# Hybrid attention and mLSTM layer on one core: the first stage with transposes, gate rows fetched two heads ahead, compression blocks split straight from PSUM, compression steps between projection tiles

## The chip, the cores and the metric

The kernel runs on one core of a Trainium2 chip. The core has TensorE (PE: matmuls, with PEld loading the stationary operand beside it), VectorE (DVE), ScalarE (ACT), GpSimd (POOL) and SyncE (SP, which here only issues DMAs). The metric is the device time of one execution in microseconds; lower is better. All times below are in microseconds.

## The reference

```
h = rms_norm(x, mix_norm_pre)                       # x: 512 x 1024
q, kc, vc, ks, vs, kw, vw, gt, mq, mk, mv, mi, mf, mo = split(h @ w_in)
k_cmp, v_cmp = compress_blocks(kc, ...), compress_blocks(vc, ...)
#   blocks of 32 tokens, stride 16, + pos; silu(blocks @ w1) @ w2
o = native_sparse_attention(q, k_cmp, v_cmp, ks, vs, kw, vw, sigmoid(gt), rel_bias)
mq, mk = split(silu(causal_conv(concat(mq, mk), conv_w) + conv_b))
hm = mlstm(mq, mk, mv, mi + bias, log_sigmoid(mf + bias))   # 4 heads, gated decay
y = concat(o, sigmoid(mo) * rms_norm(hm) * mlstm_norm) @ w_out
x = x + rms_norm(y);  x = x + rms_norm(cross_attention(rms_norm(x), mem))
x = x + rms_norm(swiglu_ffn(rms_norm(x)))
```

Everything is float32, and the changed parts lie before the attention: the first norm, the product with w_in, the convolution, the compression of key and value blocks, and the mLSTM heads.

## The kernel before

Matmuls run on pairs of fp32r numbers. `split(hi, lo, src, eng)` writes the rounded high half on ACT (a copy) and the rest on DVE or POOL (a subtract); `mm3` then makes three matmuls, high by low, low by high, high by high. In the names below, whi and wlo are the halves of a projection weight, hTh and hTl those of the transposed normed input H, wah and wal those of the gate weights, w1s both halves of a piece of the compression weights, Xb both halves of the compression input.

The first stage is a block in which the order of the instructions on every engine is the written one (manual_schedule). For each of the four rows i of 128 tokens it takes the sum of squares on ACT (`square_of`), the factor rstd on DVE and POOL (`factor_of`, rs_e and rs_r), turns the row into H by eight matmuls, four to a PSUM bank bk_pn (`turn_row`, two calls), splits the banks (`parts_of`) and multiplies H by the gate and window-value weights, 24 matmuls of 288 columns to a row (bk_A, `gates_and_v(i, 0)` and `(i, 1)`). `keep_a` takes bk_A's results out. After the block comes `mlstm_v`, 96 matmuls of 512 columns (bk_mv).

After it a scheduler that works when the kernel is built, and not a fixed list, sets each engine's order: it takes the program in the order of PLAN["order"], by priority, as operands and buffers become available in its own model. In that string c0, c1 (convolution input), m0, m2 (output gate), kc, ks (keys and values), q0 are projections, and each name stands once for each of the tiles that it has. A tile is 24 matmuls into a bank bk_dT. Lk, Lv load the compression weights; Ck, Cv are steps of the compression (four matmuls of 512 columns each into bk_hb); S0 to S3 are the scores of an mLSTM head (bk_ms) and O0 to O3 its output (bk_mn, bk_mt). Every name of `PLAN["m0"]` and the like says for each tile whether POOL (p) or DVE (v) makes wlo.

Buffers are rings: the weights whi/wlo, five of the eight w1s of the keys and all w1s of the values use one of 4 buffers ("W"), the other w1s and the rows of x one of 4 ("T"), 512-column temporaries one of 16 ("G"), the large pairs such as hT one of 6 ("S"). A new writer waits until the reader of the buffer that it takes is done. PSUM has 2 banks for projection tiles, 3 for scores and bk_hb, 2 for turns, 1 for values.

`ev_conv` takes a tile of c0 or c1 out of PSUM and begins the convolution with the newest tap; `ev_mo` takes m0 and m2 tiles out (tanh) and scales them; `ev_kcvc` builds the compression input of kc's two tiles; `mlstm_scores` makes an mLSTM head's decay weights from rb, a row of rd (a DRAM scratch) broadcast to all partitions by a 256 KB DMA.

## Time and profile before

| what | value |
| --- | --- |
| median of 3 runs | 849.62 (848.80 to 850.38) |
| the profiled execution, its own time | 849.66 |
| its span, first to last instruction | 847.9 |
| mean granted TensorE clock, share of full | 0.992 |
| PE busy | 821.3 (97%), 4870 matmuls |
| DVE busy | 542.3 (64%) |
| ACT busy | 425.1 (50%) |
| POOL busy | 299.2 (35%) |

The profile is one execution; 1.8 of its own time lies outside the span. Busy shares are means over stages with different limits. A granted clock of 1.00 is 2.4 GHz and 0.50 is 1.2 GHz. Where PE idles, the trace names what it waited for. PE's matmuls overlap, so the distance between two starts is what a matmul costs, not its printed duration.

### The profile page before, as it was taken

The numbers are of one execution on the slowest core, as the hardware profiler recorded it, in microseconds if no ns is written. First come the engines' busy times: TensorE is split into PE (matmuls) and PEld (weight loads), VectorE is DVE, ScalarE is ACT, GpSimd is POOL, SyncE is SP. The second block draws the span as 40 slices with busy tenths as digits, with TensorE's granted clock in tenths as the row PEclk, the third lists the DMA queues.
The fourth block names the chain that finished last, engine by engine and source line by source line (L and its number), as shares of the span: only waits on it lengthen the run. The fifth ranks groups of instructions, "written<-read, shape, count | busy, mean of one in ns | idle before, by whom it ended". The sixth has DMA issues, their size and how long they took to land.

```text
span 847.9 us, 12708 instructions
## 1 busy us (share of the span) xinstructions
PE 821.3 (97%) x4870; PEld 707.7 (83%) x4870; DVE 542.3 (64%) x934; ACT 425.1 (50%) x840; POOL 299.2 (35%) x224
## 2 busy tenths in 40 slices
PE   8999989999999999999999999999999999999997
PEld 5977767886688978778888889999999999888885
DVE  5738696697879835843453769988877885224323
ACT  5524565858867743743452556444444444324311
POOL 2043332355537542511320111444444444323320
PEclk9999999998999999999999999999999999999999
DMA  8371323221203232251341033333333322232102
GB/s 246 95 229 63 100 66 107 99 69 50 76 1 100 94 133 73 70 179 53 137 160 50 0 125 105 121 111 111 111 113 113 108 106 100 100 100 100 49 26 75
DMA packets 67763, 83.18 MB, mean 98 GB/s; under 512 B 4368, under 2 KB 53873, under 8 KB 67702
## 3 DMA queue, kind: packets, MB, share of 16 engines
q1 hardware_dynamic: 64574, 77.97, 28.3%
q10 hardware_dynamic: 3128, 4.40, 1.6%
q8 instruction: 38, 0.62, 0.3%
q14 instruction: 23, 0.19, 0.1%
HBM read 80.24 MB, written 2.12 MB: 97 GB/s over the span
## 4 chain that ended last, share of the span: by engine, by line
PE 78%; DVE 7%; ACT 3%; issue 1%; POOL 1%; DVEq 0%; ACTq 0%; POOLq 0%
PE bk_X L1301 5%; PE bk_X L1302 5%; PE bk_X L1303 5%; PE bk_ff L286 5%; PE bk_ff L288 5%; PE bk_ff L287 5%; PE bk_dT L286 4%; PE bk_dT L287 4%; PE bk_dT L288 4%; PE bk_pv L1027 3%; PE bk_dN L287 3%; PE bk_dN L286 3%; PE bk_dN L288 3%; PE bk_Z L1301 2%; PE bk_Z L1302 2%; PE bk_Z L1303 2%
## 5 line engine op out<-in xcount | busy, mean ns | idle before, releaser
L166 ACT ACTIVATE whi<-raw 128x1024 fp32r<-128x1024 f32 (+1 forms) x80 | 76.8, 968 | 63.4 <-PE bk_dT L286 27.8
L167 DVE TENSOR_TENSOR wlo<-raw,whi 128x1024 fp32r<-128x1024 f32 x41 | 54.2, 1323 | 81.5 <-PE bk_ff L287 43.0
L167 POOL TENSOR_TENSOR wlo<-raw,whi 128x1024 fp32r<-128x1024 f32 x23 | 55.8, 2428 | 106.4 <-ACT whi L166 104.6
L166 ACT ACTIVATE wh<-raw 128x1024 fp32r<-128x1024 f32 x64 | 67.3, 1057 | 49.3 <-PE bk_X L1301 16.1
L167 POOL TENSOR_TENSOR wl<-raw,wh 128x1024 fp32r<-128x1024 f32 x19 | 55.5, 2921 | 97.5 <-ACT wh L166 70.2
L286 PE MATMUL bk_dT<-hTh,wlo 128*128 128x512 f32 x192 | 76.9, 401 | 1.1 <-DVE wlo L167 0.8
L287 PE MATMUL bk_dT<-hTl,whi 128*128 128x512 f32 x192 | 76.3, 397 | 0.0
L288 PE MATMUL bk_dT<-hTh,whi 128*128 128x512 f32 x192 | 76.1, 396 | 0.0
L167 DVE TENSOR_TENSOR wl<-raw,wh 128x1024 fp32r<-128x1024 f32 x45 | 64.6, 1440 | 9.2 <-ACT wh L166 9.2
L167 POOL TENSOR_TENSOR gs<-gf,gs 128x512 fp32r<-128x512 f32 x22 | 32.4, 1478 | 65.9 <-ACT gs L166 65.9
L1302 PE MATMUL bk_X<-A,wh 128*128 128x256 f32 x192 | 54.5, 284 | 1.0 <-DVE A L167 1.0
L1301 PE MATMUL bk_X<-A,wl 128*128 128x256 f32 x192 | 54.4, 283 | 0.4 <-ACT A L166 0.4
L1303 PE MATMUL bk_X<-A,wh 128*128 128x256 f32 x192 | 54.3, 283 | 0.0
L287 PE MATMUL bk_ff<-wlo,gs 128*128 128x512 f32 x128 | 49.8, 389 | 0.0
L288 PE MATMUL bk_ff<-whi,gs 128*128 128x512 f32 x128 | 49.6, 389 | 0.0
L1301 PE MATMUL bk_X<-AS,wl 128*128 128x256 f32 x160 | 45.6, 285 | 2.4 <-ACT u L1356 2.3
L286 PE MATMUL bk_ff<-whi,gs 128*128 128x512 f32 x128 | 47.4, 389 | 0.0
L997 POOL TENSOR_SCALAR s<-s,acf 128x128 f32<-128x128 f32 (+3 forms) x32 | 36.5, 1151 | 26.7 <-PE bk_tr L1012 15.9
L1302 PE MATMUL bk_X<-AS,wh 128*128 128x256 f32 x160 | 44.9, 281 | 0.0
L1301 PE MATMUL bk_Z<-AS,wl 128*128 128x256 f32 x160 | 44.9, 281 | 0.0
L1303 PE MATMUL bk_X<-AS,wh 128*128 128x256 f32 x160 | 44.9, 281 | 0.0
L1303 PE MATMUL bk_Z<-AS,wh 128*128 128x256 f32 x160 | 44.9, 280 | 0.0
(376 smaller groups left out, 2535.2 us busy)
## 6 DMA issues: line engine op xcount, KB each, us to landing
raw<-in_w_gate_up_dram SPq DMA_DIRECT2D x22, 1024.0 KB, 6.5
raw<-in_w_down_dram SPq DMA_DIRECT2D x11, 1024.0 KB, 4.9
raw<-in_w_xkv_dram SPq DMA_DIRECT2D x8, 1024.0 KB, 5.1
raw<-in_w_in_dram SPq DMA_DIRECT2D x7, 1024.0 KB, 5.3
raw<-in_w_out_dram SPq DMA_DIRECT2D x4, 1024.0 KB, 5.1
raw<-in_w_xq_dram SPq DMA_DIRECT2D x4, 1024.0 KB, 5.4
raw<-in_w_xo_dram SPq DMA_DIRECT2D x4, 1024.0 KB, 5.1
raw<-in_w_in_dram SPq DMA_DIRECT2D x6, 512.0 KB, 4.7
```

The costliest lines, as they stand in the source:

```text
L166: first = nc.scalar.activation(hi, src, AF.Copy)
L167: second = (eng or nc.vector).tensor_tensor(lo, src, hi.bitcast(F32), op=OP.subtract)
L286: nc.tensor.matmul(o, lhsT=wl, rhs=xh, start=start, stop=False)
L287: nc.tensor.matmul(o, lhsT=wh, rhs=xl, start=False, stop=False)
L288: return nc.tensor.matmul(o, lhsT=wh, rhs=xh, start=False, stop=stop).ins
L997: ENG[on].tensor_scalar(s[:, 0:n], s[:, 0:n], c, None, op0=OP.mult)
L1027: nc.tensor.matmul(o, lhsT=v, rhs=pTs[br][q][:, j], start=(br, j, q) == mms[0], stop=(br, j, q) == mms[-1])
L1301: nc.tensor.matmul(o, lhsT=wl[:, k, c], rhs=A.hi(n, k), start=st, stop=False, skip_group_check=True)
L1302: nc.tensor.matmul(o, lhsT=wh[:, k, c], rhs=A.lo(n, k), start=False, stop=False, skip_group_check=True)
L1303: nc.tensor.matmul(o, lhsT=wh[:, k, c], rhs=A.hi(n, k), start=False, stop=stop and k == 3, skip_group_check=True)
```

## The change

1. First stage. The row is scaled by rstd and gain in one DVE instruction (`norm_half`), and turned by a PE transpose with the identity in place of a matmul by diag(rstd). The multiplication by the gain alone (xg) and the building of the diagonal (mt) are left out. x's second row is loaded ahead of the gate weights, the third ahead of their second half. The calls stand in a new order: row 1 is turned between the two halves of row 0's gates_and_v, and the squares and factors come earlier.
2. Gate rows. The store of rd and the loads of rb go through SP's queue instead of ACT's, and rb is loaded two heads ahead (`load_rb`).
3. `ev_conv` and `ev_mo`: a DVE tensor_scalar becomes an ACT Identity with scale and bias, in ev_conv from PSUM.
4. `ev_kcvc`: Xb is split straight from PSUM with a stride of 16, four ACT copies and four DVE subtracts of 64 x 496 to a tensor, in place of eight DVE adds of 64 x 248, four ACT copies and four DVE subtracts. The position goes into the 32nd column of the block list and is added back through `fold` and `every`.
5. The value weights of the compression take two "G" buffers in place of one "W" in every second piece.
6. PLAN["order"]: two Ck stand between the tiles of m0, two before c1; Cv stand one by one between S1, m2, S2 and m2.

The diff, cut to its core:

```diff
-        "order": "c0 Lk c0 Lv kc m0 m0 Ck Ck Ck Ck c1 kc S0 O0 c1 "
-                 "S1 Cv Cv Cv Cv m2 S2 m2 O2 ks O1 ks q0 S3 q0 O3",
+        "order": "c0 Lk c0 Lv kc m0 Ck Ck m0 Ck Ck c1 kc S0 O0 c1 "
+                 "Cv S1 Cv m2 Cv S2 Cv m2 O2 ks O1 ks q0 S3 q0 O3",
...
         "w1tk": "WTWTWTWW",
-        "w1tv": "WWWWWWWW",
-        "xb": "vv",
+        "w1tv": "GWGWGWGW",
...
     nc.sync.dma_start(cc[:, 0:128], a["consts"][:, 0:128])
+    load_x(1)
     raw_a = [load_a(0)]
-    load_x(1)
+    load_x(2)
     raw_a.append(load_a(1))
-    load_x(2)
     load_x(3)
...
-    xg, dg, turned, bank_a = {}, {}, {}, {}
+    xn, factor, turned, bank_a = {}, {}, {}, {}
     def square_of(i):
-        ss = dg[i] = small([P, 1], "ss", 4)
+        ss = factor[i] = small([P, 1], "ss", 4)
         nc.scalar.activation(sgran((P, D), BF16, name="junk"), res(i), AF.Square, scale=1.0 / 32.0, accum_out=ss)
-    def gain_of(i, g):
+    def factor_of(i):
+        factor[i] = rstd_of(factor[i], 1)
+    def norm_half(i, g):
         if g == 0:
-            xg[i] = x4([P, D], name="xg")
+            xn[i] = x4([P, D], name="xn")
         c = slice(512 * g, 512 * g + 512)
-        nc.vector.tensor_tensor(xg[i][:, c], res(i)[:, c], g_in[g], op=OP.mult)
-    def factor_of(i):
-        r = rstd_of(dg[i], 1)
-        dg[i] = small([P, P], "mt1")
-        nc.vector.tensor_scalar(dg[i], ident, r, None, op0=OP.mult)
+        nc.vector.scalar_tensor_tensor(xn[i][:, c], res(i)[:, c], factor[i], g_in[g], op0=OP.mult, op1=OP.mult)
...
             kk = 4 * g + k
-            nc.tensor.matmul(b[:, 128 * k:128 * k + 128], lhsT=xg[i][:, 128 * kk:128 * kk + 128], rhs=dg[i],
-                             start=True, stop=True)
+            nc.tensor.transpose(b[:, 128 * k:128 * k + 128], xn[i][:, 128 * kk:128 * kk + 128], ident)
...
         nc.scalar.activation(g_in[1], spread[1], AF.Copy)
-        gain_of(0, 0)
+        square_of(1)
         factor_of(0)
-        turn_row(0, 0)
-        gain_of(0, 1)
-        turn_row(0, 1)
+        for g in range(2):
+            norm_half(0, g)
+            turn_row(0, g)
         warm_up(2)
-        parts_of(0, 0)
+        factor_of(1)
+        for g in range(2):
+            parts_of(0, g)
         split_a(0)
-        parts_of(0, 1)
+        norm_half(1, 0)
         split_a(1, 2, 3)
         raw_m = [load_m(0)]
+        norm_half(1, 1)
         gates_and_v(0, 0)
         for g in range(2):
-            gain_of(1, g)
+            turn_row(1, g)
+        square_of(2)
         split_a(4, 5)
-        square_of(1)
-        factor_of(1)
+        factor_of(2)
+        for g in range(2):
+            parts_of(1, g)
         split_a(6, 7)
...
         gates_and_v(0, 1)
-        square_of(2)
         for g in range(2):
-            turn_row(1, g)
-        for g in range(2):
-            gain_of(2, g)
-        for g in range(2):
-            parts_of(1, g)
+            norm_half(2, g)
         for i in range(1, NT):
             then = i + 1 < NT
-            if then:
-                factor_of(i + 1)
             gates_and_v(i, 0)
...
             done = gates_and_v(i, 1)
-            last = (done, *keep_a(i - 1))
             if i + 2 < NT:
                 square_of(i + 2)
-                for g in range(2):
-                    gain_of(i + 2, g)
+                factor_of(i + 2)
             if then:
...
                     parts_of(i + 1, g)
+            if i + 2 < NT:
+                for g in range(2):
+                    norm_half(i + 2, g)
+            last = (done, *keep_a(i - 1))
     with ExitStack() as behind:
...
     rd = dr.tile([4, 512], F32, name="rd")
-    nc.scalar.dma_start(rd, rr)
+    nc.sync.dma_start(rd, rr)
+    rbs = {}
+    def load_rb(h):
+        if h < 4:
+            rbs[h] = sgran(name="rb")
+            nc.sync.dma_start(rbs[h], rd[h:h + 1, :].to_broadcast([P, 512]))
+    for h in range(2):
+        load_rb(h)
     nc.vector.tensor_tensor(ir, ir, br_, op=OP.subtract)
...
             nc.scalar.activation(u, b, AF.Copy)
-            nc.vector.tensor_scalar(y, u, cw(c, 3), cb(c), op0=OP.mult, op1=OP.add)
+            nc.scalar.activation(y, b, AF.Identity, scale=cw(c, 3), bias=cb(c))
             for w in range(3):
...
             nc.scalar.activation(sg[c], b, AF.Tanh, scale=0.5)
-            nc.vector.tensor_scalar(sg[c], sg[c], 1.0, hn(c), op0=OP.add, op1=OP.mult)
+            nc.scalar.activation(sg[c], sg[c], AF.Identity, scale=hn(c), bias=hn(c))
         return f
...
         nc.vector.scalar_tensor_tensor(kB[r], zc[2 + h // 2][r], 0.0625, kA[r].bitcast(F32), op0=OP.mult, op1=OP.subtract)
-        rb = mgran(name="rb")
-        nc.scalar.dma_start(rb, rd[h:h + 1, :].to_broadcast([P, 512]))
+        rb = rbs[h]
         dg = mgran((P, NT, P), name="dg")
...
             sT.append(W[:, c0:c0 + n])
+        load_rb(h + 2)
         return sT
...
         n = "kv"[j]
-        Xr = [sgran((P, 8, 64), name="Xr") for _ in range(2)]
-        for X in Xr:
-            nc.gpsimd.memset(X, 0.0)
+        X = Xb[n] = slot([P, 2, 8, 2, 64], F32R, name="Xb")
+        nc.gpsimd.memset(X[:, :, :, :, 63:64].bitcast(F32), 0.0)
+        pos = posT[n].rearrange("p (q j o) -> p q j o", q=2, o=1)
+        split(X[:, :, :, 0, 31:32], X[:, :, :, 1, 31:32], pos)
+        full, to = [], []
         for kv in range(2):
             for r in range(2):
-                full = b[64 * kv:64 * kv + 64, :].rearrange("p (b j r) -> p r j b", r=2, j=8)
-                pt = posT[n][64 * r:64 * r + 64, :]
-                for q in range(2):
-                    nc.vector.tensor_tensor(Xr[q][64 * r:64 * r + 64, :, 32 * kv:32 * kv + 31],
-                                            full[:, r, :, q:q + 31],
-                                            pt[:, 8 * q:8 * q + 8].rearrange("p (j o) -> p j o", o=1).to_broadcast([64, 8, 31]),
-                                            op=OP.add)
-        Xb[n] = []
-        for X in Xr:
-            for g in range(2):
-                B = gran((P, 4, 2, 64), F32R, name="Xb")
-                split(B[:, :, 0, :], B[:, :, 1, :], X[:, 4 * g:4 * g + 4, :], engines("xb")[g])
-                Xb[n].append(B)
+                one = b[64 * kv:64 * kv + 64, r:r + 1]
+                full.append(bass.AP(tensor=one.tensor, offset=one.offset, ap=[one.ap[0], [16, 2], [2, 8], [16, 31]]))
+                to.append(X[64 * r:64 * r + 64, :, :, :, 32 * kv:32 * kv + 31])
+        for q in range(4):
+            nc.scalar.activation(to[q][:, :, :, 0], full[q], AF.Copy)
+        for q in range(4):
+            nc.vector.tensor_tensor(to[q][:, :, :, 1], full[q], to[q][:, :, :, 0].bitcast(F32), op=OP.subtract)
...
     nc.vector.tensor_tensor(fold, ident[:, 0:64], ident[:, 64:128], op=OP.add)
+    every = small([P, 1], "every", 1)
+    nc.vector.tensor_copy(every, fold[:, 31:32])
+    nc.vector.tensor_scalar(fold, fold, every, None, op0=OP.add)
...
         for s in range(8):
-            take = x4 if PLAN["w1t" + n][s] == "T" else w4
-            w = take([P, 2, 2, 256], F32R, name="w1s")
-            split(w[:, :, 0, :], w[:, :, 1, :], w1r[n, s // 4][s % 4], engines("w1" + n)[s])
+            take = PLAN["w1t" + n][s]
+            if take == "G":
+                w = [gran((P, 2, 256), F32R, name="w1s") for _ in range(2)]
+                for k in range(2):
+                    split(w[k][:, 0, :], w[k][:, 1, :], w1r[n, s // 4][s % 4][:, k], engines("w1" + n)[s])
+            else:
+                t = (x4 if take == "T" else w4)([P, 2, 2, 256], F32R, name="w1s")
+                split(t[:, :, 0, :], t[:, :, 1, :], w1r[n, s // 4][s % 4], engines("w1" + n)[s])
+                w = [t[:, k] for k in range(2)]
             for k in range(2):
                 kk = 2 * s + k
-                nc.tensor.matmul(hb[n], lhsT=Xb[n][kk // 4][:, kk % 4].rearrange("p q b -> p (q b)"),
-                                 rhs=w[:, k].rearrange("p q c -> p (q c)"), start=kk == 0, stop=kk == 15)
+                nc.tensor.matmul(hb[n], lhsT=Xb[n][:, kk // 8, kk % 8].rearrange("p q b -> p (q b)"),
+                                 rhs=w[k].rearrange("p q c -> p (q c)"), start=kk == 0, stop=kk == 15)
             if s == 7:
```

Order of the instructions. First PE in the first stage, where row 1 is turned (bk_pn is a turn of eight; bk_A is a step of three matmuls; each row names engine, line and operands). Before:

```order
L286 MATMUL bk_A<-wah,hTl 128x288
L287 MATMUL bk_A<-wal,hTh 128x288
L288 MATMUL bk_A<-wah,hTh 128x288
L491 MATMUL bk_pn<-mt_227,xg 128x128 x8
L286 MATMUL bk_A<-wah,hTl 128x288
L287 MATMUL bk_A<-wal,hTh 128x288
L288 MATMUL bk_A<-wah,hTh 128x288
```

24 bk_A matmuls precede the turn, so it stands behind both halves of row 0. After:

```order
L285 MATMUL bk_A<-wah,hTl 128x288
L286 MATMUL bk_A<-wal,hTh 128x288
L287 MATMUL bk_A<-wah,hTh 128x288
L488 MATMUL bk_pn<-cc,xn 128x128 x8
L285 MATMUL bk_A<-wah,hTl 128x288
L286 MATMUL bk_A<-wal,hTh 128x288
L287 MATMUL bk_A<-wah,hTh 128x288
```

Twelve bk_A matmuls precede it now: row 1 is turned in the middle of row 0.

Next PE at the end of m0's first tile, bk_dT, of which the last two matmuls are shown (names carry the number of the buffer; hb is a compression step, ms a score of an mLSTM head). After:

```order
L286 MATMUL bk_dT_819<-hTl_95,whi_815 128x512
L287 MATMUL bk_dT_819<-hTh_93,whi_815 128x512
L892 MATMUL bk_hb_847<-w1s_848,Xb_801 128x512 x2
L892 MATMUL bk_hb_847<-w1s_853,Xb_801 128x512 x2
L761 MATMUL bk_ms_1030<-qm_1019,kmA_1020 128x512
L761 MATMUL bk_ms_1039<-qm_1019,kmA_1020 128x384
L892 MATMUL bk_hb_847<-w1s_858,Xb_801 128x512 x2
L892 MATMUL bk_hb_847<-w1s_863,Xb_801 128x512 x2
L762 MATMUL bk_ms_1030<-qm_1019,kmB_1025 128x512
```

and behind these 24 matmuls of m0's second tile begin (bk_dT_872, whi_868). Before, this place held m0's second tile at once, and the four Ck came behind both tiles:

```order
L287 MATMUL bk_dT_864<-hTl_95,whi_860 128x512
L288 MATMUL bk_dT_864<-hTh_93,whi_860 128x512
L880 MATMUL bk_hb_892<-w1s_893,Xb_814 128x512 x2
L880 MATMUL bk_hb_892<-w1s_898,Xb_814 128x512 x2
L756 MATMUL bk_ms_1057<-qm_1044,kmA_1045 128x512
L757 MATMUL bk_ms_1057<-qm_1044,kmB_1050 128x512
L756 MATMUL bk_ms_1066<-qm_1044,kmA_1045 128x384
L757 MATMUL bk_ms_1066<-qm_1044,kmB_1050 128x384
```

So eight bk_hb and four bk_ms stand between the tiles now, and the other eight behind the second.

Last ACT ahead of whi of m2's first tile (whi_1294 before, whi_1229 after; sT, qm, kmA, hnat, mt are mLSTM work, Xb and w1s compression). Before:

```order
L709 ACTIVATE u_1174<-bk_dT_1149 128x512
L166 ACTIVATE w1s_1241<-w1_758 128x2x256
L787 ACTIVATE mt1_1105,mss_1087<-hnat_1086 128x128
L787 ACTIVATE mt1_1116,mss_1087<-hnat_1086 128x128
L166 ACTIVATE w1s_1246<-w1_763 128x2x256
L166 ACTIVATE w1s_1251<-w1_764 128x2x256
L166 ACTIVATE w1s_1256<-w1_765 128x2x256
L166 ACTIVATE w1s_1261<-w1_766 128x2x256
L166 ACTIVATE whi_1294<-raw_1292 128x1024
```

After:

```order
L769 ACTIVATE sT_1288<-rb_1059,ub_614 128x128 x3
L165 ACTIVATE w1s_1167<-w1_755 128x2x256
L821 ACTIVATE Xb_1007<-bk_dT_982 64x16x31 x4
L165 ACTIVATE w1s_1222<-w1_757 128x2x256
L168 ACTIVATE kcmp_651<-bk_cmp_932 128x2x32
L914 DMA w2_1336<-in_cmp_w2_v_dram 128x2x64
L831 ACTIVATE qm_1274<-zc_970 64x512
L793 ACTIVATE mt1_1080,mss_1062<-hnat_1061 128x128
L791 ACTIVATE hnat_1061<-bk_mn_1082,dn_1086 128x128
L165 ACTIVATE whi_1229<-raw_1227 128x1024
```

The w1s copies of the last four pieces and u of c1's second tile no longer stand ahead of it; three exps, two w1s, four Xb copies, which now read PSUM, kcmp, qm, mt and hnat do.

## Rows read from the trace of the kernel before

**Rows 1.** Busy table of the page: us, share of span, instructions.

```profile
PE 821.3 (97%) x4870; PEld 707.7 (83%) x4870; DVE 542.3 (64%) x934; ACT 425.1 (50%) x840; POOL 299.2 (35%) x224
```

**Rows 2.** Windows: from:to, length, busy PE, PEld, DVE, ACT, POOL, clock, DMA, GB/s.

```profile
58.70:143.37 84.67, 78.70 (x359) 61.01 (x357) 67.08 (x127) 46.52 (x104) 32.10 (x32) 0.98 0.31 93
...
125.00:128.40 3.40, 3.40 (x8) 1.98 (x7) 3.40 (x6) 1.68 (x3) 1.39 (x2) 0.50 0.00 0
...
193.30:200.10 6.80, 6.15 (x21) 4.47 (x20) 5.71 (x18) 6.70 (x18) 4.90 (x4) 0.50 0.36 108
```

**Rows 3.** Timeline of PE, first stage: start, duration, engine, line, operation [idle before, releaser].

```profile
17.33 0.40 PE L287 MATMUL bk_A<-wal,hTh 128*128 128x288 f32 x1 [0.77 <-POOL wal L167]
...
18.46 1.95 PE L491 MATMUL bk_pn<-mt,xg 128*128 128x128 f32 x16
...
20.93 0.40 PE L286 MATMUL bk_A<-wah,hTl 128*128 128x288 f32 x1 [0.52 <-DVE hTl L167]
...
21.16 0.29 PE L287 MATMUL bk_A<-wal,hTh 128*128 128x288 f32 x1
...
22.48 0.29 PE L288 MATMUL bk_A<-wah,hTh 128*128 128x288 f32 x1
...
34.40 0.29 PE L288 MATMUL bk_A<-wah,hTh 128*128 128x288 f32 x1
```

**Rows 4.** Timeline of PE, transposes at the end of attention's first units.

```profile
227.92 1.04 PE L254 MATMUL bk_pn<-cc,xn 128*128 128x128 f32 x8
```

**Rows 5.** Timeline of DVE and POOL, first stage.

```profile
13.19 1.89 DVE L480 TENSOR_TENSOR xg<-xin,gain 128x512 f32<-128x512 f32 x2
...
15.96 0.56 POOL L236 TENSOR_TENSOR rs_r<-rs_e,mhalf 128x1 f32<-128x1 f32 x1 [2.03 <-DVE rs_e L232]
...
16.48 1.55 POOL L167 TENSOR_TENSOR wal<-raw,wah 128x288 fp32r<-128x288 f32 x2
```

**Rows 6.** Timeline of PE, projection tiles.

```profile
58.70 0.48 PE L286 MATMUL bk_dT<-hTh,wlo 128*128 128x512 f32 x1
...
68.73 0.39 PE L287 MATMUL bk_dT<-hTl,whi 128*128 128x512 f32 x1
...
90.79 1.20 PE L880 MATMUL bk_hb<-w1s,Xb 128*128 128x512 f32 x4 [0.89 <-DVE w1s L167]
...
118.83 0.38 PE L756 MATMUL bk_ms<-qm,kmA 128*128 128x256 f32 x1 [1.75 <-DVE sT L766]
...
124.78 3.62 PE L880 MATMUL bk_hb<-w1s,Xb 128*128 128x512 f32 x8 [1.61 <-DVE w1s L167]
...
128.99 0.50 PE L286 MATMUL bk_dT<-hTh,wlo 128*128 128x512 f32 x1 [0.58 <-DVE wlo L167]
...
143.37 0.48 PE L286 MATMUL bk_dT<-hTh,wlo 128*128 128x512 f32 x1
```

**Rows 7.** Timeline of ACT, POOL and DVE, weight splits.

```profile
93.30 1.06 ACT L166 ACTIVATE whi<-raw 128x1024 fp32r<-128x1024 f32 x1 [0.30 <-PE bk_hb L880]
...
118.43 0.61 ACT L166 ACTIVATE w1s<-w 128x512 fp32r<-128x512 f32 x1
...
102.87 2.38 POOL L167 TENSOR_TENSOR wlo<-raw,whi 128x1024 fp32r<-128x1024 f32 x1 [7.70 <-ACT whi L166]
...
127.73 1.20 DVE L167 TENSOR_TENSOR wlo<-raw,whi 128x1024 fp32r<-128x1024 f32 x1
```

**Rows 8.** Window of ACT's work in the projections, columns as in rows 2.

```profile
108.74:118.43 9.69, 8.11 (x41) 6.32 (x40) 8.51 (x22) 9.06 (x25) 2.55 (x2) 1.00 0.32 77
```

**Rows 9.** Timeline of PE, start of attention.

```profile
192.35 0.44 PE L977 MATMUL bk_sc<-kA,qst 128*128 128x384 f32 x1 [1.15 <-DVE mx L981]
...
193.86 1.09 PE L698 MATMUL bk_pcT<-cc,pc 128*128 128x128 f32 x4 [0.55 <-DVE pc L695]
```

**Rows 10.** Adds of ev_kcvc by line (min/median/max ns), and ACT at rb.

```profile
L811 DVE TENSOR_TENSOR Xr<-bk_dT,chan x16: 398/410/420, 81.0 to 114.7; 64x248 f32<-64x248 f32 x16
...
132.94 0.99 ACT L764 ACTIVATE sT<-rb,ub 128x128 f32<-128x128 f32 x3 [1.82 <-DMA rb<-rd]
```

## Prediction

> **What bounds the kernel now.** I read the busy table first: TensorE (PE) is busy 97% of the span [rows 1], so whatever shortens the run must take out PE's own matmuls, its waits, or its time at the lower clock. Then windows, then PE's timeline in the two places that the change touches. The later two thirds (attention units, w_out, cross-attention, FFN) run without a wait worth naming and the change doesn't touch them.
>
> The first place is the first stage. Before the last matmul of bk_A PE runs turns (bk_pn, matmuls by diag(rstd)) and bk_A in one line. A turn of 8, two banks, listed as 16 halves, starts at 18.46 and costs about 2.0; bk_A's matmuls of 288 columns start 0.132 apart at full clock (21.16 to 22.48 in ten steps) [rows 3]. The waits are for wal, the low halves of the gate weights (0.77 before 17.33), and for hTl (0.52 before 20.93). The last bk_A begins at 34.40, ends at 34.69.
>
> The second place is the row of projection tiles from the first c0 matmul at 58.70 to the first ks matmul at 143.37 [rows 6]: 84.67, of which PE is busy 78.70, so 5.97 idle [rows 2]. The large idles stand before bk_hb (0.89, 1.61), bk_ms (1.75) and m2's first tile (0.58) [rows 6]: a tile or a compression step (Ck, Cv) waits for the split of its weights. After the last series the clock is half from 125.0 to 128.4 (0.50 for 3.4 us, so 1.7 of full clock) [rows 2]; the eight bk_hb in it take 3.62 [rows 6] where eight at full clock take 1.9: 512 columns start at most 0.233 apart (58.70 to 68.73 in 43 steps). Counted start to start, a wait is 0.1 to 0.2 longer than its printed idle, since PE also empties and refills. The nine places in which a step starts late by 0.24 or more (first at 83.87, last at 128.99) are late by 7.7 together, and the half clock adds 1.4. So **9.1 us** can be gained there.
>
> The third is the start of attention: PE waits 1.15 before 192.35 for mx and 0.55 before 193.86 for pc, both from VectorE (DVE) [rows 9], and a half-clock stretch follows from 193.3 to 200.1 (0.50) [rows 2].
>
> **The first stage.** A turn becomes eight transposes. The trace has the same 128x128 transpose later: eight in 1.04 [rows 4], about 0.11 apart; with 0.9 to 1.0 a turn against 2.0. The order rows put row 1's turn in the middle of row 0's bk_A, where PE waits for wal anyway. So behind row 0's second half only two turns are left. Before: from 18.46 to 34.69 = 16.2, which is 72 x 0.132 = 9.5, three turns of 2.0, 0.52 of wait and small change. After: 9.5 + 2 x 0.9 = 11.3. That is −4.9.
>
> Ahead of it, the last two wal (POOL, 16.48 for 1.55) stand behind rs_r at 15.96, which stood behind two gain multiplies of row 1 on DVE (13.19, 1.89 for the two, slow because POOL ran too) [rows 5]. After, row 1's factor comes earlier since x1 is loaded ahead of the gate weights, and the DVE no longer multiplies by the gain apart from the scale. Walking POOL, ACT and DVE through the new order with these durations, I get the end of wal 1.1 earlier. Sum **−6.0**, between −4.5 (the turn in the gap delays bk_A) and −6.5. Everything behind (bk_mv, its loads and splits) can follow: splits of wm lead PE by about 2.6 now, and the new order gets to them as much earlier. The moved keep_a and the removed diag costs lie under PE's bk_A.
>
> The price of the transposes is the largest unknown of this part. The row shows eight in 1.04, and the turns of now, eight ordinary matmuls of the same size, 2.0. I take the row of the transposes; should they cost what a turn costs now, two turns of 2.0 instead of 0.9 take back 2.2. The page "TensorE: Matmul & The Clock Gate" of the Trainium skill, section "Part 4: PE-mode transpose", speaks for the dear price: it gives about 275 ns for one transpose inside a kernel, by which a turn of eight would cost 2.2 and the whole sum below would be 2.6 smaller.
>
> **Compression blocks from PSUM.** Before, ev_kcvc adds the positions on DVE, 16 instructions of 0.41 [rows 10], and then splits; after, four ACT copies and four DVE subtracts a tensor read PSUM with the same stride, each over twice as many elements. No row shows an ACT copy with this stride. The DVE adds bound it: 0.4 if width costs nothing, 0.8 by doubling. I take 0.6. DVE is relieved of the adds and of eight 512-wide scales, since the conv's last tap and ev_mo's scale become ACT Identity, near 0.6 each as w1s, a copy of as many elements [rows 7]. This earns nothing by itself: what it costs ACT stands in wait 3 below. The position column, the added `every` and the two memsets are small and lie under PE's tiles. Gate rows: ACT waited 1.82 for rb before 132.94 [rows 10]; the store of rd and the loads of rb now stand on SP's queue, where they wait for DMAs only, and the weights of ks, the next load behind them, are needed some 15 us later. PE ran m2's second half at 132.94, so this earns nothing directly, at most ACT's 1.8.
>
> **Projections.** The new order and pools remove all of the 9.1 as it stands and set four new waits. Whi is 1.06 on ACT (0.95 apart), wlo 2.38 on POOL and 1.20 on DVE, w1s 0.61 on ACT [rows 7].
>
> (1) m0's second tile, now behind two Ck: its whi takes the buffer that m0's first tile frees at its end; 0.95 + 2.38 = 3.3 against 8 bk_hb (1.9) and four bk_ms (0.8): 0.6.
>
> (2) c1's first tile, behind the other two Ck: w1s 0.61, sg 0.5, whi 0.95, wlo 1.20 = 3.3 against 8 bk_hb and four small bk_ms, 2.4: 0.85.
>
> (3) m2's first tile. In the order of ACT (third place in the order rows) its whi is behind all that begins at c1's first tile's end: whi, u, zc, hid, then what before's ACT does in 9.06 from 108.74 to 118.43 [rows 8] (hnat, qm, kmA, ten exps, tanh, w1s, Xb), with larger Xb (+1.0) and two more mt and hnat (+0.9), and its own 1.06: 14.6, then 1.2 for wlo: 15.8. PE meanwhile has 48 matmuls of 512 columns (11.2) and some 16 small ones (1.8): 13.0. Wait 2.8, taken as **3.0 ± 1**.
>
> (4) m2's second tile: ACT has about 9 to 10 between the two whi, PE about 10.1 less the 1.2 of wlo: 0 to 2, taken as 1.1.
>
> Sum 5.55. A wait of 3 in the midst of busy matmuls is like what stood before the half clock at 125.0; I count one such stretch, +1.5 (1.7 at most). So 9.1 − 5.55 − 1.5 = **−2.0**.
>
> **Attention's start.** PE would arrive about 8 us earlier, but so does the DVE chain (its work is the same and DVE's backlog smaller): −0.5, between 0 and −2.
>
> **Sum.** −6.0 − 2.0 − 0.5 = −8.5. The profiled execution took 849.66, the median of three is 849.62, so it makes no difference: 849.6 − 8.5 = **841.1**.
>
> **Rivals.**
>
> (a) Nothing of waits 3 and 4 appears, since ACT gets the copies done in gaps that I counted as full. Then 1.45 of 9.1 remains: −6.0 − 7.6 − 0.5 = 835.5. For it: PE's waits before were for DVE, which is relieved. Against: the order on ACT.
>
> (b) The projections gain nothing: the same waits plus a longer half-clock stretch (as 193.3 to 200.1, 3.4 instead of 1.5) and one more short one (+1.7): 9.1 − 5.55 − 5.1 = −1.5 turns to +1.5, 849.6 − 6.0 + 1.5 = 845.1.
>
> (c) bk_mv comes before the split weights: the lead of 2.6 is used up and 2.6 of the first stage's gain is given back, 843.7. For it: wm's pieces come from ACT and DVE one at a time behind the new splits and factors, and their loads depend on buffers, not on PE alone. Against: ACT and DVE are idle between bk_A's rows.
>
> (c') Transposes cost what turns cost now: 841.1 + 2.2 = 843.3. Only the row of another stage speaks against it. (The price that the Trainium skill's page gives would come out here.)
>
> (d) Slower: half-clock stretches follow every one of the four new waits, and each is of the long kind (3.4). Nine us of gain are needed to be lost: 4 x 3.4 = 13.6 in place of 1.5 gives 849.6 − 8.5 + 12.1 = 853.2; it decides from three long ones on. For: near 193 it fell where the waits were of only 1.15 and 0.55 [rows 2, 9]. Against: the stretch from 58.70 to 143.37 has 0.98 as its mean and just one half-clock piece, though PE waits eight times in it [rows 2].
>
> (e) No part reaches the end: the first stage's gain is taken back by loads and the projections as in (b): 849.6 + 1.5 − 0.5 = 850.6.
>
> **How the numbers follow.** Forecast 0.46 (its own range 838.6 to 843.6, by the bounds of wait 3, of the clock and of the first stage); (a) 0.17; (b) 0.16; (c) 0.05; (c') 0.04; (d) 0.07; (e) 0.05. The range leaves out the ends of (a), (d) and (e): 834.5 to 846.5. A measurement of this kernel tells about 0.2%, 1.7 us, from no change; (e) is within it, (d) beyond, the rest faster, with a little of (b) moved to no change: 0.86, 0.06, 0.08.
>
> **What would show it.** The last bk_A at about 28.6 instead of 34.7; turns of 8 in about 0.9; first ks matmul near 135 (143.4 − 8); PE waits before m0's second tile on POOL wlo of 0.6, before c1's first on DVE wlo of 0.85, and before m2's first tile of about 3 behind whi, with a clock under 1.00 in the windows that follow; no ACT wait on rb; no TENSOR_SCALAR in ev_conv; Xb copies on ACT of 0.6. I am wrong if the m2 wait is absent (a), if strided copies cost over 1.5, or if bk_mv waits for its weights (c).

## The result: slower by 0.55%, and the profile after

The changed kernel takes 853.69 (median of 6 runs, 851.86 to 855.62) against 849.21 for the kernel before; the ratio is 1.0055 with an interval of 1.0038 to 1.0072. It was forecast at 841.1 with 834.5 to 846.5: wrong, and on the other side. The profiled execution of the changed kernel is its slowest, 855.62 with a span of 853.8, 6.0 more than the one of before. Counted from the start of each execution, the first c0 matmul comes 2.0 later (60.73), the first ks matmul 3.3 later (146.69), the first bk_pcT 5.7 later (199.53) and the first matmul of w_out 7.2 later; 1.3 of this comes back behind it.

The busy table of the page, as in [rows 1]:

```profile
PE 816.7 (96%) x4838; PEld 703.7 (82%) x4838; DVE 537.3 (63%) x911; ACT 432.5 (51%) x854; POOL 303.4 (36%) x225
```

PE is busy 4.6 less in a span that is 5.9 longer: it idles 37.1 instead of 26.6. First the timeline of PE in the first stage, as in [rows 3]:

```profile
15.04 0.44 PE L287 MATMUL bk_A<-wah,hTh 128*128 128x288 f32 x1
15.28 1.88 PE L488 MATMUL bk_pn<-cc,xn 128*128 128x128 f32 x8
...
20.26 0.49 PE L286 MATMUL bk_A<-wal,hTh 128*128 128x288 f32 x1 [0.54 <-POOL wal L166]
...
23.43 0.45 PE L287 MATMUL bk_A<-wah,hTh 128*128 128x288 f32 x1
...
28.40 0.37 PE L285 MATMUL bk_A<-wah,hTl 128*128 128x288 f32 x1 [2.03 <-DVE gl L508]
...
30.06 1.04 PE L488 MATMUL bk_pn<-cc,xn 128*128 128x128 f32 x8
...
33.38 0.37 PE L285 MATMUL bk_A<-wah,hTl 128*128 128x288 f32 x1 [0.71 <-DVE gl L508]
...
36.49 0.29 PE L287 MATMUL bk_A<-wah,hTh 128*128 128x288 f32 x1
```

The last bk_A begins at 36.49, not at 28.3 (its forecast end of 28.6 less its own 0.29). A turn of eight does cost what the forecast took, 1.04. But twice PE waits for gl, the last instruction of keep_a, which frees the bank that the next row's bk_A writes; keep_a now stands behind parts_of and norm_half. The last wal comes at 20.26 instead of 18. And the clock is at its lower level where it wasn't: bk_A's matmuls start 0.24 apart and the turn takes 1.88 up to 17.1 (before the change only until 12.4), and again from 20.3. POOL and ACT show why wal is late: its wah stands behind the hTh of row 1, which waits for the turn.

```profile
17.20 0.60 ACT L165 ACTIVATE hTh<-bk_pn 128x512 fp32r<-128x512 f32 x1 [0.23 <-PE bk_pn L488]
17.69 0.77 ACT L165 ACTIVATE wah<-raw 128x288 fp32r<-128x288 f32 x2
...
18.20 2.00 POOL L166 TENSOR_TENSOR wal<-raw,wah 128x288 fp32r<-128x288 f32 x2 [1.94 <-ACT wah L165]
```

Windows of the changed kernel, columns as in [rows 2], and behind them two of the kernel before that answer to the fifth and sixth:

```profile
20.30:23.70 3.40, 3.40 (x15) 3.39 (x16) 0.52 (x2) 0.00 (x0) 0.55 (x1) 0.52 0.68 198
60.73:146.69 85.96, 77.39 (x346) 61.07 (x343) 59.27 (x100) 52.02 (x112) 34.18 (x32) 0.96 0.31 95
88.00:95.00 7.00, 6.83 (x23) 5.54 (x24) 5.21 (x7) 6.42 (x18) 2.92 (x2) 0.76 0.44 116
124.00:131.50 7.50, 6.56 (x22) 5.21 (x23) 7.05 (x12) 2.97 (x8) 7.25 (x7) 0.77 0.00 0
146.69:199.53 52.84, 49.52 (x268) 41.69 (x269) 35.78 (x123) 35.84 (x96) 19.16 (x18) 0.98 0.27 80
199.53:299.96 100.43, 98.29 (x632) 78.90 (x633) 85.09 (x259) 76.05 (x208) 54.43 (x40) 0.97 0.18 59
```

```profile
143.37:193.86 50.49, 47.80 (x260) 40.32 (x260) 37.65 (x122) 32.26 (x91) 19.67 (x17) 0.99 0.27 89
193.86:292.73 98.87, 98.28 (x629) 79.12 (x629) 82.56 (x255) 76.91 (x209) 54.74 (x40) 0.97 0.19 59
```

From c0 to ks PE idles 8.57 where it idled 5.97, and there are two pieces with a lowered clock (7.0 at 0.76 and 7.5 at 0.77, 1.7 of full clock each) where there was one of 1.7. That is 4.3; the stretch grew only by 1.3, in part because 14 small matmuls of the mLSTM outputs and of the compression (six bk_mn, four bk_ht, four bk_cmp) slipped behind ks, where PE is busy 1.7 more. Taken over the three stretches up to w_out PE idles 14.0 instead of 9.3. These are the large waits of the projections, as in [rows 6], and of attention's start, as in [rows 9]:

```profile
88.17 1.61 PE L892 MATMUL bk_hb<-w1s,Xb 128*128 128x512 f32 x4 [2.73 <-ACT whi L165]
...
101.22 0.50 PE L285 MATMUL bk_dT<-hTh,wlo 128*128 128x512 f32 x1 [0.60 <-DVE wlo L166]
...
124.94 0.50 PE L285 MATMUL bk_dT<-hTh,wlo 128*128 128x512 f32 x1 [3.68 <-DVE wlo L166]
...
137.15 0.47 PE L761 MATMUL bk_ms<-qm,kmA 128*128 128x512 f32 x1 [1.22 <-DVE sT L771]
...
194.99 0.36 PE L989 MATMUL bk_sc<-kA,qst 128*128 128x256 f32 x1 [0.78 <-DVE dn L786]
...
196.95 0.44 PE L989 MATMUL bk_sc<-kA,qst 128*128 128x384 f32 x1 [1.48 <-DVE mx L993]
...
198.36 0.69 PE L989 MATMUL bk_sc<-kA,qst 128*128 128x384 f32 x1 [0.80 <-DVE mx L993]
...
201.74 1.12 PE L798 MATMUL bk_mt<-cc,hnat 128*128 128x128 f32 x4 [0.70 <-DVE hnat L797]
```

Behind the wait of 3.68 the clock falls, as the forecast had it. This wait is not ACT's alone. ACT ends whi of m2's first tile at 122.01, but DVE begins wlo only at 123.67: it is at the subtracts of Xb until 121.87, and those of w1s, kcmp and qm stand behind them, ahead of wlo.

```profile
119.14 2.73 DVE L823 TENSOR_TENSOR Xb<-bk_dT,Xb 64x496 fp32r<-64x496 f32 x4 [1.55 <-ACT Xb L821]
...
120.96 1.05 ACT L165 ACTIVATE whi<-raw 128x1024 fp32r<-128x1024 f32 x1
...
123.67 1.21 DVE L166 TENSOR_TENSOR wlo<-raw,whi 128x1024 fp32r<-128x1024 f32 x1
```

The wait of 2.73 was not in the forecast. It is put down to a whi, but this is not what Ck needs, and the load of Ck's stationary operand, Xb, begins before that whi ends at 88.16. The timelines of ACT, DVE and PEld show the chain:

```profile
82.92 2.34 ACT L821 ACTIVATE Xb<-bk_dT 64x496 fp32r<-64x496 f32 x4
...
85.29 2.73 DVE L823 TENSOR_TENSOR Xb<-bk_dT,Xb 64x496 fp32r<-64x496 f32 x4 [1.55 <-ACT Xb L821]
...
87.10 1.06 ACT L165 ACTIVATE whi<-raw 128x1024 fp32r<-128x1024 f32 x1
...
88.13 0.91 PEld L892 LDWEIGHTS bk_hb<-w1s,Xb 128*128 128x128 f32 x4 [3.13 <-issue]
```

The first of the four subtracts begins only behind the last of the four copies, the last one ends at 88.02, and PE starts 0.15 later. With Ck directly behind m0's first tile, Xb, which nobody waited for before, is late.

### The profile page after: what moved, and what is told of

It reads as the page before. It is cut to its first block, busy times and chain, and to the rows that moved or that the text cites. A ratio compares the mean times of both kernels' runs of the same rounds, so it can differ in the third digit from the quotient of the medians.

```text
span 853.8 us, 12625 instructions
## 1 busy us (share of the span) xinstructions
PE 816.7 (96%) x4838; PEld 703.7 (82%) x4838; DVE 537.3 (63%) x911; ACT 432.5 (51%) x854; POOL 303.4 (36%) x225
## 4 chain that ended last, share of the span: by engine, by line
PE 80%; DVE 10%; ACT 5%; issue 3%; POOL 2%; ACTq 0%; DVEq 0%; POOLq 0%
PE bk_X L1313 5%; PE bk_X L1314 5%; PE bk_ff L285 5%; PE bk_ff L287 5%; PE bk_ff L286 5%; PE bk_X L1315 5%; PE bk_dT L285 5%; PE bk_dT L286 4%; PE bk_dT L287 4%; PE bk_pv L1039 3%; PE bk_dN L286 3%; PE bk_dN L285 3%; PE bk_dN L287 3%; PE bk_tr L1024 2%; PE bk_Z L1313 2%
## 5 line engine op out<-in xcount | busy, mean ns | idle before, releaser
L166 DVE TENSOR_TENSOR wl<-raw,wh 128x1024 fp32r<-128x1024 f32 x45 | 66.9, 1493 | 9.1 <-ACT wh L165 9.1
L285 PEld LDWEIGHTS bk_dT<-hTh,wlo 128*128 128x128 f32 x192 | 36.5, 190 | 14.4 <-DVE wlo L166 6.2
L1314 PE MATMUL bk_X<-AS,wh 128*128 128x256 f32 x160 | 44.3, 277 | 0.0
```

The source lines that it names most:

```text
L166: second = (eng or nc.vector).tensor_tensor(lo, src, hi.bitcast(F32), op=OP.subtract)
L285: nc.tensor.matmul(o, lhsT=wl, rhs=xh, start=start, stop=False)
L1314: nc.tensor.matmul(o, lhsT=wh[:, k, c], rhs=A.lo(n, k), start=False, stop=False, skip_group_check=True)
```

## The experiments

Each ran in five rounds beside the kernel before, whose median lay between 848.86 and 849.06 in every group.

| run | median | ratio to before, interval |
| --- | --- | --- |
| first_only | 848.22 | 0.9991 (0.9976 to 1.0005) |
| first_old | 855.01 | 1.0065 (1.0052 to 1.0079) |
| keep_mid | 853.26 | 1.0044 (1.0023 to 1.0066) |
| warm4 | 854.34 | 1.0056 (1.0040 to 1.0071) |
| order_old | 849.74 | 1.0021 (1.0002 to 1.0040) |
| kc_old | 853.27 | 1.0052 (1.0035 to 1.0070) |
| ident_old | 854.83 | 1.0064 (1.0044 to 1.0084) |
| rb_old | 859.28 | 1.0119 (1.0101 to 1.0137) |
| order_m0 | 856.54 | 1.0081 (1.0054 to 1.0109) |
| order_cv | 852.13 | 1.0035 (1.0020 to 1.0050) |
| order_only | 858.26 | 1.0127 (1.0099 to 1.0154) |
| best1 | 851.57 | 1.0029 (1.0012 to 1.0045) |
| first_fix | 841.81 | 0.9917 (0.9902 to 0.9932) |
| kc_only | 856.51 | 1.0092 (1.0074 to 1.0110) |
| ident_only | 853.00 | 1.0053 (1.0037 to 1.0068) |
| rb_only | 856.06 | 1.0087 (1.0069 to 1.0106) |
| after_fix | 848.35 | 0.9996 (0.9979 to 1.0013) |
| first_keep | 844.76 | 0.9948 (0.9930 to 0.9966) |

**The first stage alone, and undone.** first_only is the kernel before with the diff's loads, norm_half, turn_row and the calls in their new order; first_old is the changed kernel without them.

> The kernel before with the new first stage alone (loads of x, transposes, new order of the calls), the rest as before. Theory A: the first stage loses by itself, about +2 at the first c0 matmul (60.7 against 58.7 in the changed kernel's trace), by the wait for keep_a's DVE gl (2.0 + 0.7) and by half clock until 17.1 and from 20.3 to 23.7: total about +2, 851. Rival B: the first stage gains as forecast where nothing else is changed (-6): 843.

> The changed kernel with the old first stage. Theory A: the loss of the first stage goes away and what the projections and attention's start lose stays (+1.3 and +2.3 in the trace): about 2 less than the changed kernel, 851.5, still slower than before. Rival B, that the later losses follow from the first stage's end (loads and buffers that come later): back to 849 or less.

Alone the first stage does nothing that can be measured; undoing it makes the changed kernel no faster, so that both forecasts for first_old were missed. The loss of 4.5 is thus not the first stage's, against theory A, and a gain of 6 isn't there either, against rival B. In the trace of first_only the same waits for gl stand (2.02 and 0.69), behind the longer one the clock is at its lower level, and its last bk_A ends at 34.8, as the one of the kernel before (34.7):

```profile
24.91 0.58 PE L286 MATMUL bk_A<-wah,hTl 128*128 128x288 f32 x1 [2.02 <-DVE gl L509]
```

```profile
24.80:28.20 3.40, 3.29 (x14) 3.30 (x15) 0.00 (x0) 0.00 (x0) 0.00 (x0) 0.50 0.03 5
```

**Its two waits.** keep_mid and warm4 are the changed kernel with

```diff
                     parts_of(i + 1, g)
+            last = (done, *keep_a(i - 1))
             if i + 2 < NT:
                 for g in range(2):
                     norm_half(i + 2, g)
-            last = (done, *keep_a(i - 1))
```

and with

```diff
-        warm_up(2)
+        warm_up(4)
         nc.scalar.activation(g_in[0], spread[0], AF.Copy)
```

> The changed kernel with keep_a moved between parts_of and norm_half. Theory A: gl is done before the multiplies by rstd and gain, the wait of 2.0 before bk_A at 28.4 shrinks to about 0.6 (norm_half's 1.4 is out of the chain), the one at 33.4 stays at 0.7: -1.4 at the last bk_A, total about 852.2. Rival: the wait turns into one for hTl or xn of the next row, no gain.

> The changed kernel with four dummy matmuls instead of two behind the gain's, which fill the idle 1.06 before the first turn. Theory A: the half clock up to 17.1 is owed to this gap; with PE busy the clock rises at about 12.5 as before, 4.6 of half clock saved, 2.3 less at the last bk_A and perhaps the second half-clock stretch (20.3 to 23.7, 1.7) too: 850 to 851.5. Rival: the clock rises no earlier, since the transposes or the short bk_A don't hold it: no change.

In keep_mid the wait of 2.03 falls to 0.70, as expected, and the last bk_A ends at 33.1; in warm4 the turn of row 1 takes 1.03 and the clock is up in time, and the last bk_A ends at 33.8. So neither rival's mechanism came, and yet neither median moved beyond the uncertainty; warm4's 850 to 851.5 was missed. In the profile of keep_mid the projections swallow what came: c0 begins 3.7 earlier than in the changed kernel and ks no earlier, mostly since the stretch between them has a clock of 0.92 instead of 0.96.

```profile
57.02:146.82 89.80, 79.92 (x345) 62.58 (x343) 58.59 (x100) 53.02 (x113) 34.34 (x32) 0.92 0.30 91
```

In the profile of warm4 they do not: c0 comes 3.0 earlier, ks 3.3 and w_out 3.0, and behind it 1.3 is given back.

**Parts of the rest, undone one at a time.** order_old has the old string of PLAN["order"]; kc_old the old ev_kcvc, comp and w1tv; ident_old the two DVE tensor_scalars; rb_old the loads of rb and the store of rd on ACT:

```diff
ident_old
-            nc.scalar.activation(y, b, AF.Identity, scale=cw(c, 3), bias=cb(c))
+            nc.vector.tensor_scalar(y, u, cw(c, 3), cb(c), op0=OP.mult, op1=OP.add)
...
rb_old
-        rb = rbs[h]
+        rb = mgran(name="rb")
+        nc.scalar.dma_start(rb, rd[h:h + 1, :].to_broadcast([P, 512]))
```

> The changed kernel with the old PLAN order (both tiles of m0, then four Ck; S1, then four Cv, then m2). Theory A, the order sets the new waits: the wait of 2.7 before the first Ck (Xb is just being split when PE comes) falls to under 1, the 3.7 before m2's first tile goes, since its whi no longer stands behind S1, Xb and w1s at once; attention's start as in the kernel before: about 5 less than the changed kernel, 848 to 849. Rival B, ACT's load is the cause whatever the order: waits of the same size stand at the Ck and Cv after the tiles, 852 to 854.

> The changed kernel with the old ev_kcvc (adds on DVE, Xb in four G tiles, w1s of the values all in W). Theory B (copies of 0.58 with stride on ACT ahead of the weights' splits): the wait before m2's first tile falls by 1 to 1.5 and the one before the first Ck changes little: 851.5 to 852.5. Theory A (order): no change or slower, since DVE gets 6.6 more work in the same order: 854 to 856.

> The changed kernel with the conv's last tap and ev_mo's scale back on DVE. ACT loses eight instructions of 0.75 (they measured 0.77 and 0.80, where 0.6 was forecast): before m2's first tile one of them stands, so the wait falls by up to 0.7; DVE gains eight. Theory A: within 1 of the changed kernel, 853 to 854.5. Theory B: 852.

> The changed kernel with rb loaded inside mlstm_scores on ACT's queue and rd stored there. Both theories: no wait of PE hangs on rb; if the loads two heads ahead matter, S1 and S2 come 1 to 2 later and the kernel is 1 slower; forecast 853 to 855.

In the medians the old order takes back nearly all of the loss, as theory A had it. Its trace is less clear. The wait before the first Ck and the one before m2 go, but m0's second tile waits 3.46 instead, for the subtracts of Xb, and the first Cv 2.79 for w1s, much as rival B had it:

```profile
85.74 0.63 PE L285 MATMUL bk_dT<-hTh,wlo 128*128 128x512 f32 x1 [3.46 <-DVE Xb L823]
...
122.22 0.50 PE L892 MATMUL bk_hb<-w1s,Xb 128*128 128x512 f32 x1 [2.79 <-POOL w1s L166]
```

From c0 to ks it takes 86.4, no less than the changed kernel. Its profiled span is 6.4 shorter, but 3.5 of this lies before c0, where both kernels have the same code; what is left is mostly the 2.6 from ks to w_out.

In kc_old the wait before m2 falls from 3.68 to 1.06, and one of 2.53 for w1s comes at a later Cv, so the total stays. This does not show the share of ACT's copies: four to a tensor stand on ACT there too, shorter ones, and PE has eight bk_hb and eight bk_ms between c1's last tile and m2's first, where the changed kernel has neither.

```profile
116.50 1.32 ACT L166 ACTIVATE Xb<-Xr 128x256 fp32r<-128x256 f32 x4
```

```profile
125.24 0.50 PE L286 MATMUL bk_dT<-hTh,wlo 128*128 128x512 f32 x1 [1.06 <-DVE wlo L167]
```

ident_old can't be told from the changed kernel, as theory A expected. rb_old was missed: 5.6 slower than the changed kernel, not the 1 allowed.

**The halves of the order.**

```diff
order_m0
-        "order": "c0 Lk c0 Lv kc m0 Ck Ck m0 Ck Ck c1 kc S0 O0 c1 "
+        "order": "c0 Lk c0 Lv kc m0 m0 Ck Ck Ck Ck c1 kc S0 O0 c1 "
...
order_cv
-                 "Cv S1 Cv m2 Cv S2 Cv m2 O2 ks O1 ks q0 S3 q0 O3",
+                 "S1 Cv Cv Cv Cv m2 S2 m2 O2 ks O1 ks q0 S3 q0 O3",
```

> The changed kernel with the first half of the order undone (m0 m0, then four Ck); Cv stand as changed. Theory A2, the steps Cv between S1, m2, S2 and m2 are what costs: the waits of 3.8 and 1.4 around m2 stay; before the Ck the wait of 2.9 goes and one for m0's second tile of 3.6 (as with the old order) comes: no change, 853 to 854. Rival A1, the steps Ck between m0's tiles cost: 850.

> The changed kernel with the second half of the order undone (S1 Cv Cv Cv Cv m2 S2 m2); Ck stand as changed. Theory A2: the waits of 3.8 and 1.4 at m2 go, one of about 2 before the Cv comes, attention's start is earlier by 2 to 3: 849.5 to 850.5. Rival A1: 853.

With the first half undone the kernel is no faster (its median is 3 higher), against A1, which had 850. With the second half undone it is faster by 1.6, which is within the uncertainty and lies between A2 and A1; the wait before m2 goes there, and one of 2.79 stands before a Cv. So the steps Ck alone are not what costs; that the steps Cv are, is not shown, and the halves don't add to 4.

**Each part alone, and a first mixture.** order_only, kc_only, ident_only and rb_only are the kernel before with that one part; best1 is the kernel before with the first stage as in keep_mid and warm4, the gate rows and the ACT scales.

> The kernel before with the new order alone. Theory A: the order costs by itself about 4, whatever stands around it: 852 to 854. Rival: the order costs only together with the copies and scales that the change puts on ACT: 848 to 850.

> The kernel before with the new first stage (keep_a between parts_of and norm_half, four dummy matmuls before the first turn), gate rows on SP two heads ahead and the ACT scales; old order, old ev_kcvc. If the parts add: first stage -0.7 alone and -1 to -2 with its two waits taken out, rb and scales -1 to 0: 846 to 847.5. Rival, the gains before the projections are given back in the waits for split weights: 849.

> The kernel before with the new ev_kcvc (and G tiles for the values' w1s) alone, old order. Theory: the four copies on ACT stand ahead of whi of m0's second tile, where the run with the old order waited 3.6, but the Ck come sooner: within 1.5 of before, 848 to 850.5. Rival, the split from PSUM gains what the new order costs: 845 to 847.

> The kernel before with the ACT Identity for conv and output gate alone. DVE loses up to 3.6 in the chain that ends in the score matmuls of S1 (the wait of 1.9 at 116.7), ACT gains 0.8 a tile: 847.5 to 849. Rival: ACT's queue sets the waits, 850.

> The kernel before with the gate rows on SP two heads ahead alone. In the old order only one wait of ACT on rb (1.8) is seen: no change, 848.5 to 849.5. Rival: the exps come earlier and the wait of 1.9 at 116.7 goes: 847.

Each of the four parts costs 4 to 9 by itself, and the whole change costs 4.5. All five forecasts were missed on the slow side, the rivals too: the mixture best1 is 2.6 slower than the kernel before. In order_only the first Ck waits for Xb by the old, longer way:

```profile
89.12 2.08 PE L880 MATMUL bk_hb<-w1s,Xb 128*128 128x512 f32 x4 [5.52 <-DVE Xb L167]
```

That is twice the 2.73 of the full change, which fits a split from PSUM that pays for half of what the order costs there, but kc_only, with this split in the old order, is 7.6 slower than before. In rb_only no wait of PE hangs on rb, and yet a Cv waits 3.35 for w1s on DVE: the scheduler gave ACT and DVE other orders.

A good part of these costs is the clock. These are the windows from c0 to ks of kc_only, rb_only, order_only and ident_only; the kernel before has 84.67 at 0.98 [rows 2].

```profile
58.89:151.92 93.03, 82.47 (x359) 64.90 (x357) 63.79 (x115) 49.88 (x111) 32.60 (x33) 0.91 0.28 84
58.59:148.23 89.64, 80.98 (x359) 62.82 (x357) 69.73 (x126) 46.22 (x103) 35.26 (x32) 0.94 0.31 92
58.13:147.26 89.13, 78.06 (x341) 60.34 (x339) 66.59 (x119) 45.32 (x101) 32.62 (x32) 0.96 0.30 89
60.31:146.84 86.53, 79.42 (x360) 61.52 (x357) 62.88 (x120) 52.01 (x113) 33.98 (x33) 0.96 0.30 91
```

A window of 93.03 at 0.91 has lost some 8.4 of full clock, and the one of before 1.7. So most of what kc_only has more is lower clock, and in order_only less than half of it.

**The first stage mended.** first_fix is first_only with three lines moved or changed, first_keep with the first of them, after_fix is the changed kernel with all three:

```diff
             done = gates_and_v(i, 1)
+            last = (done, *keep_a(i - 1))
...
-            last = (done, *keep_a(i - 1))
...
+        split_a(6, 7)
         factor_of(2)
         for g in range(2):
             parts_of(1, g)
-        split_a(6, 7)
...
-        warm_up(2)
+        warm_up(4)
```

> The kernel before with the new first stage, in which three places are mended: keep_a stands right behind gates_and_v(i, 1) as before, the last two wal are made ahead of row 1's parts, four dummy matmuls stand before the first turn. Theory A (the forecast -6 was taken back by the wait for keep_a's bank, 2.0 + 0.7, by the wal behind row 1's turn, about 1, and by half clock): the last bk_A ends at 30 to 31.5 instead of 34.7, total 845 to 846.5. Rival: transposes and splits leave nothing, the loss moves to another wait (hTl, wm): 848.

> The kernel before with the new first stage, where keep_a alone is put back right behind gates_and_v(i, 1); the wal behind row 1's turn and the two dummy matmuls stay. Theory: of the 6.4 between the first stage alone (848.2) and mended (841.8) the waits for keep_a's bank are 2.7 and what half clock follows them 1 to 2: 844 to 845.5. Rival: the half clock at the start and the late wal carry most: 847.

> The changed kernel with the three mendings of the first stage that gave -7 on the kernel before. Theory: first stage and projections add, so the changed kernel less 6 to 7: 847 to 848. Rival: the changed projections swallow an earlier start in their waits, as they did in keep_mid and warm4 (first c0 matmul 3 earlier, end no earlier): 851 to 853.

first_fix beats both kernels, by 0.83% against the one before, and its own forecast. Its timeline of PE has no wait left from 14.0 to the last bk_A, and its window from c0 to ks has the full clock:

```profile
14.07 1.03 PE L489 MATMUL bk_pn<-cc,xn 128*128 128x128 f32 x8
...
18.39 1.04 PE L489 MATMUL bk_pn<-cc,xn 128*128 128x128 f32 x8
...
22.62 1.03 PE L489 MATMUL bk_pn<-cc,xn 128*128 128x128 f32 x8
...
28.14 0.29 PE L288 MATMUL bk_A<-wah,hTh 128*128 128x288 f32 x1
```

```profile
52.43:137.46 85.03, 77.96 (x360) 60.06 (x357) 67.51 (x127) 46.60 (x104) 32.10 (x32) 1.00 0.32 94
```

The last bk_A ends at 28.43, the forecast's 28.6, and c0 starts 6.3 earlier than before; the projections take their 85 as before, and the end comes 7.1 earlier. Of the 6.4 from first_only to first_fix, keep_a alone brings 3.5 (first_keep), as expected. In after_fix the mending brings 5.3: the parts nearly add, and it is as fast as the kernel before. Its profiled execution is its slowest, 852.49: c0 starts 8.3 earlier than in the changed kernel, and the stretch to ks takes 3.7 more with a clock of 0.92, as in keep_mid.

## Why the prediction was wrong

**First stage.** The prices were right: a turn of eight is 1.04. By the 275 ns that the Trainium skill's page ("TensorE: Matmul & The Clock Gate", "Part 4: PE-mode transpose") gives for one bf16 transpose inside a kernel, a turn would take an estimated 2.2. The trace does not agree: one lasts 0.27 in it, but the next starts 0.11 behind it. The step that failed is "The moved keep_a and the removed diag costs lie under PE's bk_A". bk_A has two banks, so the row after next waits for keep_a, and behind norm_half it is late by 2.0 and 0.7. Likewise "I get the end of wal 1.1 earlier" was wrong: wah 6 and 7 were moved behind row 1's hTh, which waits for the turn, and wal ended at 20.2 instead of the forecast's 16.9 (18.0 before). And the lower clock up to 17.1 wasn't counted at all. first_fix shows that these three are all that was missing: with them out, c0 comes 6.3 earlier, for the 6.0 of the forecast. The share of the dummy matmuls in this is not known, and in first_only the clock was up in time without them; keep_a has 3.5 of the 6.4 at the end.

**Projections.** That the new order and pools "remove all of the 9.1 as it stands and set four new waits", −2.0, became +1.3 in the profile, with the work that slipped behind ks to come. Of the four, c1's first tile (0.60 for 0.85) and m2's first (3.68 for 3.0) came about in size and in place; in m2's the forecast had ACT's queue alone, and 1.66 of it is DVE's, between whi and wlo. m0's second did not come, and the one at m2's second tile came on sT at 137.15, 1.22 for 1.1. Left out was a fifth, the first Ck waiting 2.73 for Xb, and with it a second piece of lowered clock, 1.7. I had priced the copies (0.58 each for 0.6) but not followed who waits for the last one: the sentence "This earns nothing by itself: what it costs ACT stands in wait 3 below" is the step.

**Attention's start.** −0.5 became +2.3 up to bk_pcT and +1.6 in the units behind it: 153.3 from ks to w_out instead of 149.4. Of the +2.3 PE is busy 1.7, with the matmuls that slipped and a clock of 0.98 for 0.99, and idle 0.6; the +1.6 is all idle. The mLSTM heads are late since m2 (the bk_mt that began at 190.29 begins at 201.74) and bring their dn and hnat to DVE there, beside attention's own mx. With the second half of the order undone this stretch takes 149.2 (order_cv, 145.00 to 294.16), with the whole of it 150.7 (order_old, 143.70 to 294.35): this loss belongs in part to the order. Only in part: kc_old and ident_old, with the changed order, take 151.4.

**The sum and the rivals.** Against the forecast's −8.5 the profiled execution has +6.0: 8.0 of the difference from the first stage, 3.3 from the projections, 2.9 from attention's start, 1.6 from its units, less 1.3 that comes back behind. (d) named the sign and, at 853.2, nearly the time, but only its mechanism's half is there: the clock falls behind two of the new waits, for 1.7 each and not 3.4, so that its number is near by luck. (c) and (c') did not happen; (b) and (e) come nearest, with the first stage's gain not there and the projections no better.

**What stays open.** That the gate rows, the ACT scales and the split from PSUM each cost 4 to 8 by themselves, while undoing them in the changed kernel costs −0.4 to +5.6, no single wait explains. Each of these edits makes the scheduler order ACT and DVE anew (first_only leaves their order as it was), and in every such trace other waits for w1s, Xb and sT stand between 80 and 140; whether the order before is merely a lucky one was not tried. The clock of all executions points to a common term. Its mean over the span has a median of 0.993 in the kernel before and 0.988 in the changed one; 0.005 of some 850 is 4.3, an estimate near the whole loss of 4.5. first_only, first_fix and first_keep, with the projections of before, have 0.993 too, and all other runs 0.984 to 0.992. That the waits lose the clock, and by it the time, is not shown: no run changes one without the other.

## What to carry to other kernels

Where an order is written out by hand, follow each moved call to the buffer that it frees: keep_a cost nothing where it stood, and a few lines below it cost 2.7 of waits and, in first_only, a lowered clock behind them. Where a scheduler makes the order from the whole program, measure parts alone and together, since here four parts that cost 4 to 9 each cost 4.5 together. And take a change apart before dropping it: the one part with a real gain, 7.1, was hidden by three lines.

## What the runs showed of the hardware

The clock's rise in the first stage is not the same in every profiled execution of the same code. The turn of row 1 took 1.88 in the profile of the changed kernel, 1.03 in first_only and 1.04 in order_old, which have the same first stage. warm4 had 1.03 as well, so that its two dummy matmuls are not shown to do anything; keep_mid, without them, had 1.91, and so had best1, with them. ACT copies of 64 x 496 from PSUM with a stride of 16 took 0.58, DVE subtracts of the same shape 0.67. An ACT Identity with scale and bias per partition took 0.75 to 0.81 where a plain copy of the same 128 x 512 takes 0.6.
